# First attention of a two-layer backbone: emptying the value product's bank with two ScalarE copies and two VectorE additions, and taking the reciprocals on GpSimd

## The chip, the cores and the metric

One core of a Trainium2 chip runs the whole program. The metric is the device time of one execution in microseconds (us). The engines are TensorE (PE, with its weight loads shown apart as PEld), VectorE (DVE), ScalarE (ACT), GpSimd (POOL) and SyncE (SP), which issues most of the DMAs. Each engine executes its own list of instructions in order; where an instruction waits for another engine, everything behind it on its list waits too.

## The reference

A backbone of two layers over 1024 latent tokens and 256 context tokens, width 1024, float32. Layer 0 is a windowed attention with 16 query heads in 4 groups and a sink logit for each head, layer 1 a latent attention; each is wrapped in a norm, a modulation and a gated residual. The change lies in layer 0 alone:

```
def attend_block(args):                      # one block of 128 queries
    s_loc = einsum("bqhgd,bkhd->bhgqk", q, k) * scale     # 3 blocks of keys, masked
    s_ctx = einsum("bqhgd,bchd->bhgqc", q, kc) * scale    # 256 context keys
    p = softmax_with_sink(concatenate([s_loc, s_ctx]), sink_b)
    return einsum(p[..., :3 * BLOCK], v) + einsum(p[..., 3 * BLOCK:], vc)
...
yx = (ox * silu(gx)) @ w_out
```

The softmax divides by the sum of the exponentials and the sink's; the kernel does the division after the product with the values.

## The kernel before

Products are made in three passes of split numbers (`split` writes a high and a low part, `mm3` runs high·high, low·high, high·low at L126 to L128). Layer 0's attention works in 40 units, numbered 0 to 39 here: ten tiles of 128 queries (in the order 2, 0, 3, 1, 4, 5, ..., 9, where tiles 0 and 1 are context) times four head groups. A unit has four heads and `m` chunks of 128 keys: 2 for context tiles, 4 for tiles 2 and 9, 5 for the others. The steps of a unit, with the names used below:

- **scores** (`score`, L584 on PE): per head two or four matmuls into one of two bank pairs, (0,1) or (2,3); then on DVE L595 adds the mask and takes the minimum (an instruction "ISA" or CUSTOM_DVE, and a small one that reads its accumulator), and on ACT L598 takes the exponential and the sum of the row.
- **denominators** (`post`, `post2`): L602 on POOL, L603 on ACT, L607 on POOL, the reciprocal L608 on DVE, and L610 on POOL, which spreads the four reciprocals over 256 columns.
- **transposes** of a chunk (`T`, L615 on PE, four of 128x128) into bank 6 or 7, which ACT (cast L121) and DVE (subtraction L122) empty into a high and a low part.
- **value products** (`PV`, L625, two matmuls of 128x512 for each chunk) into bank 5. V holds its high and low part beside each other in the stationary operand, so that the product's upper and lower 64 partitions hold two parts that have to be added. All units use this one bank: `psv = Banks(5)`.
- **emptying the bank** (`fin`): four ACT copies of 64x256 (L635 and L636, twice each) from bank 5 into two buffers, `o` and `o2`.
- **finishing** (`fin2`): two transposes of the spread reciprocals (L644, into bank 0 or 2 by turns: the first bank of a pair of the scores), an ACT copy of them (L646), then on POOL the sum `o + o2` (L648), two multiplications (L649, L650), a cast and a subtraction (L652, L653) that make the operand of the output projection. The last unit does these five on DVE (`fast=True`).
- **output projection** of a finished tile (`outproj`, L126 to L128 into bank 4, DVE L673, POOL L674) is fed between the units' chunks.

What order the instructions take on each engine is set by a scheduler when the program is built: it places each by its priority and its estimate of when operands and banks come free. A later part of the kernel (layer 1's attention) is ordered by hand. Weights of the output projection are loaded and split during the first units (`wo_load`, the casts L121 and subtractions L122 from `arena_f`).

Of the kernel before, what the change touches and what calls it, by code (L numbers as in the profile page):

```python
# [13 lines left out]
ALU = mybir.AluOpType  # L14
# [33 lines left out]
def shp(ap, *dims):  # L48
    n = 1
    for d in dims:  # L50
        n *= d
    ap = ap[:, 0:n]
    if len(dims) == 1:
        return ap
    names = "abcdefg"[: len(dims)]
    kw = {c: d for c, d in zip(names[1:], dims[1:])}
    return ap.rearrange("p (" + " ".join(names) + ") -> p " + " ".join(names), **kw)
# [3 lines left out]
def kernel(ctx: ExitStack, tc: tile.TileContext, t, out, dbg=None):  # L61
    nc = tc.nc
# [6 lines left out]
    F = cpool.tile([128, F_KB * KB], F32, name="arena_f")  # L69
# [26 lines left out]
    def sm(n):  # L96
        o = _so[0]
        _so[0] += n
        assert _so[0] <= 480
        return small[:, o : o + n]  # L100
# [39 lines left out]
    sel2 = sm(2)  # L140
    mhalf = sm(1)
    nc.vector.memset(mhalf, -0.5)
    const = sm(2)
    nc.vector.memset(const[:, 0:1], 1.0)
    nc.vector.memset(const[:, 1:2], 0.0)
# [367 lines left out]
    ytmp = Ring(F, [12], 512)  # L513
    wstg = Ring(F, [4, 6, 12], 512)
    rbr = Ring(F, [42, 47], 256)
    or1, or2, rtr = (Ring(F, [o, o - 5], 256) for o in (43, 44, 45))
    Pr = Ring(F, [14 + 2.5 * i for i in range(8)], 640)
    gr = Ring(F, [2.5, 34, 46], 256)
    xr0 = Ring(F, [4], 1024)
# [22 lines left out]
    class UnitA:  # L542
# [62 lines left out]
        def post2(self):  # L605
            den = self.den
            nc.gpsimd.tensor_add(den, den, self.esk)  # L607
            nc.vector.reciprocal(den, den)  # L608
            self.rb = rbr.next()
            nc.gpsimd.tensor_copy(shp(self.rb, 4, 64), den.unsqueeze(2).to_broadcast([128, 4, 64]))  # L610

# [18 lines left out]
        def fin(self, og):  # L630
            self.og = og
            pvv = self.pv.rearrange("p (j e q) -> p j e q", j=2, e=2)
            o, o2 = shp(or1.next(), 2, 128), shp(or2.next(), 2, 128)
            for e, a, b in ((0, 0, 64), (1, 64, 0)):
                nc.scalar.copy(o[a : a + 64], pvv[b : b + 64, :, e, :])  # L635
                nc.scalar.copy(o2[a : a + 64], pvv[a : a + 64, :, e, :])  # L636
            self.o, self.o2 = o, o2

        def fin2(self, fast=False):
            g, og = self.g, self.og  # L640
            o, o2 = self.o, self.o2
            rt = shp(prt(), 4, 128)
            for j in range(2):
                nc.tensor.transpose(rt[:, j, :], self.rb[:, j * 128 : j * 128 + 128], ident)  # L644
            rs = shp(rtr.next(), 2, 128)
            nc.scalar.copy(rs, rt[:, 0:2, :])  # L646
            eng = nc.vector if fast else nc.gpsimd
            eng.tensor_add(o, o, o2)  # L648
            eng.tensor_mul(rs, rs, self.gt)  # L649
            eng.tensor_mul(o, o, rs)  # L650
            hi = og[:, 0, 2 * g : 2 * g + 2, :]
            eng.tensor_copy(hi, o)  # L652
            eng.tensor_sub(og[:, 1, 2 * g : 2 * g + 2, :], o, hi.bitcast(F32))  # L653
# [1021 lines left out]
```

## Time and profile before

| what | value |
|---|---|
| time, median of 3 runs | 1604.39 us (1603.81 to 1604.47) |
| the profiled execution: its own time | 1606.03 us |
| its span in the trace | 1604.2 us |
| PE busy over the span | 1559.0 us, 97% |
| DVE, ACT, POOL busy | 866.1, 804.6, 734.2 us |
| layer 0's attention, units 0 to 39 | about 360 to 726 us of the span |

A profile row of a group gives the line, the engine, the operation, output <- input by name, shape, count, then busy time and mean duration in ns, then the idle time of the engine just before these instructions and what ended it. A row "X <- Y: a, b, c" of the waits says that X waited for Y for a us in total, b times, c at the longest. In the timeline a row has the start, the duration, the engine, the line and, in brackets, the idle time before it.

### The profile page before, as it was taken

What the parts mean: (1) busy time and instruction counts of PE and PEld (TensorE: products, weight loads), DVE (VectorE), ACT (ScalarE), POOL (GpSimd) and SP (SyncE); (2) the same over time, 40 slices, a digit from 0 to 9 for tenths busy, and PEclk for the clock granted to TensorE, in tenths of its full rate; (3) what the DMA queues carried; (4) which work ended last, traced back from release to release, by engine and by line L of the source; (5) the groups of instructions that cost most, each with busy time, mean ns of one, the idle gap of its engine ahead of it and who ended that gap; (6) DMA issues with size and microseconds to landing.
All of it is one profiled execution on the core that took longest, in us unless ns stands there. A gap on an engine that the chain in (4) does not pass through costs nothing.

```text
span 1604.2 us, 26843 instructions
## 1 busy us (share of the span) xinstructions
PE 1559.0 (97%) x9938; PEld 1226.8 (76%) x9938; DVE 866.1 (54%) x1589; ACT 804.6 (50%) x1558; POOL 734.2 (46%) x804
## 2 busy tenths in 40 slices
PE   7999999998999999998999999999999999999998
PEld 3787777886878888887998899766766766766587
DVE  2515551617666666667624301567666566567354
ACT  3522232349877777777523333355555555555321
POOL 1231121114554444454213340388688688789510
PEclk8999999999999999999999999999999999999999
DMA  7446766354333333317112763313323233244251
GB/s 249 167 140 196 238 201 186 100 148 119 109 109 93 96 93 93 93 57 243 49 41 85 259 198 99 103 30 81 87 82 95 66 96 96 67 128 118 63 169 66
DMA packets 147202, 192.81 MB, mean 120 GB/s; under 512 B 13936, under 2 KB 84080, under 8 KB 147072
## 3 DMA queue, kind: packets, MB, share of 16 engines
q1 hardware_dynamic: 145456, 188.94, 39.5%
q10 hardware_dynamic: 1616, 2.17, 0.4%
q8 instruction: 78, 1.28, 0.4%
q14 instruction: 52, 0.43, 0.1%
HBM read 144.90 MB, written 46.15 MB: 119 GB/s over the span
## 4 chain that ended last, share of the span: by engine, by line
PE 82%; ACT 6%; DVE 3%; issue 2%; POOL 2%; DMA 2%; SPq 0%; POOLq 0%; DVEq 0%; ACTq 0%
PE PB L126 14%; PE PB L127 14%; PE PB L128 14%; PE PB L1302 11%; PE PB L1324 8%; PE PB L1265 4%; PE PB L625 4%; PE PB L615 3%; PE PB L584 3%; ACT arena_r L121 2%; ACT arena_f L636 1%; ACT arena_f L635 1%; PE PB L181 1%; PE PB L1273 1%; ACT arena_f L598 1%
## 5 line engine op out<-in xcount | busy, mean ns | idle before, releaser
L126 PE MATMUL PB<-arena_r 128*128 128x512 f32 (+3 forms) x1496 | 509.6, 342 | 4.2 <-ACT arena_r L387 1.6
L127 PE MATMUL PB<-arena_r 128*128 128x512 f32 (+3 forms) x1496 | 503.1, 336 | 3.7 <-DVE arena_r L388 1.9
L128 PE MATMUL PB<-arena_r 128*128 128x512 f32 (+3 forms) x1496 | 501.2, 335 | 0.4 <-DVE arena_r L122 0.4
L1316 POOL TENSOR_TENSOR arena_f<-arena_f 128x512 f32<-128x512 f32 x252 | 324.6, 1288 | 79.5 <-ACT arena_f L1308 62.7
L126 PEld LDWEIGHTS PB<-arena_r 128*128 128x128 f32 x1496 | 284.0, 190 | 51.5 <-issue 12.5
L127 PEld LDWEIGHTS PB<-arena_r 128*128 128x128 f32 x1496 | 285.1, 191 | 31.4 <-DVE arena_r L388 3.4
L128 PEld LDWEIGHTS PB<-arena_r 128*128 128x128 f32 x1496 | 285.4, 191 | 28.2 <-DVE arena_r L122 0.6
L122 POOL TENSOR_TENSOR arena_r<-arena_f,arena_r 128x512 fp32r<-128x512 f32 x88 | 115.3, 1325 | 302.7 <-ACT arena_r L121 260.9
L1308 ACT ACTIVATE arena_f<-PB 128x1024 f32<-128x1024 f32 x160 | 164.1, 1027 | 108.5 <-PE PB L1302 68.9
L1267 DVE TENSOR_REDUCE arena_f<-PB 128x1 f32<-128x1024 f32 x128 | 156.1, 1219 | 86.6 <-PE PB L1265 86.5
L1302 PE MATMUL PB<-arena_r 64*128 64x512 f32 (+1 forms) x1600 | 202.4, 392 | 0.3 <-ACT arena_f L1308 0.3
L1302 PEld LDWEIGHTS PB<-arena_r 64*128 64x128 f32 (+1 forms) x1600 | 147.1, 185 | 30.6 <-ACT arena_f L1308 1.8
L595 DVE CUSTOM_DVE_ANT_0 arena_f<-PB,arena_f,small 128x640 f32<-128x640 f32 (+2 forms) x176 | 123.7, 721 | 47.6 <-PE PB L584 47.1
L122 DVE TENSOR_TENSOR arena_r<-PB,arena_r 128x512 fp32r<-128x512 f32 (+1 forms) x186 | 123.4, 673 | 39.6 <-ACT arena_r L121 38.2
L1324 PE MATMUL PB<-arena_f 128*64 128x512 f32 x640 | 144.4, 597 | 0.0
L598 ACT ACTIVATE arena_f<-arena_f,small 128x640 f32<-128x640 f32 (+2 forms) x160 | 118.9, 744 | 29.5 <-DVE small L595 28.8
L625 PE MATMUL PB<-arena_r 128*128 128x512 f32 x336 | 124.2, 440 | 8.4 <-ACT arena_f L636 7.8
L121 ACT CAST arena_r<-arena_f 128x512 fp32r<-128x512 f32 (+3 forms) x141 | 83.6, 603 | 89.5 <-DMA arena_f<-b_w_in 12.8
L121 ACT CAST arena_r<-PB 128x512 fp32r<-128x512 f32 (+1 forms) x186 | 104.9, 573 | 31.1 <-PE PB L615 28.8
L584 PE MATMUL PB<-arena_r 128*128 128x256 f32 (+1 forms) x576 | 108.2, 305 | 0.8 <-ACT arena_f L646 0.5
L1324 PEld LDWEIGHTS PB<-arena_f 128*64 128x64 f32 x640 | 43.1, 136 | 83.2 <-issue 79.9
L615 PE MATMUL PB<-ident,arena_f 128*128 128x128 f32 x672 | 105.4, 274 | 0.9 <-ACT arena_f L598 0.5
(178 smaller groups left out, 1836.2 us busy)
## 6 DMA issues: line engine op xcount, KB each, us to landing
arena_f<-ada_w SPq DMA_DIRECT2D x47, 512.0 KB, 5.3
arena_r<-q_d SPq DMA_DIRECT2D x80, 256.0 KB, 3.9
arena_r<-qn_d SPq DMA_DIRECT2D x64, 256.0 KB, 3.9
arena_r<-qr_d SPq DMA_DIRECT2D x192, 64.0 KB, 3.4
arena_f<-a_w_in SPq DMA_DIRECT2D x40, 256.0 KB, 3.4
arena_f<-x SPq DMA_DIRECT2D x16, 512.0 KB, 5.7
g_d<-arena_f SPq DMA_DIRECT2D x32, 256.0 KB, 2.2
q_d<-arena_f SPq DMA_DIRECT2D x64, 128.0 KB, 2.6
```

Source lines behind the costliest of these rows:

```text
L121: nc.scalar.copy(hi, src)
L122: (lo_eng or nc.vector).tensor_sub(lo, src, hi.bitcast(F32))
L126: nc.tensor.matmul(o, ah, bh, start=first, stop=False)
L127: nc.tensor.matmul(o, al, bh, start=False, stop=False)
L128: nc.tensor.matmul(o, ah, bl, start=False, stop=last)
L584: nc.tensor.matmul(S[:, at : at + n], qT[:, s, hq, :], kT[:, g, k : k + n], start=s == 0, stop=s == 1)
L625: nc.tensor.matmul(self.pv, V[:, self.chunks[ci], self.g, :], PT[:, s], start=ci == 0 and s == 0, stop=ci == self.m - 1 and s == 1,)
L1267: nc.vector.reduce_max(mx[:, 32 + b : 33 + b], flat, AX.X, negate=True)
L1302: nc.tensor.matmul(S[:, t], k[r, c : c + 128], q[r], start=j == 0, stop=j == 4)
L1308: nc.scalar.activation(E, self.S, AF.Exp)
L1316: eng.tensor_add(self.acc, self.acc, E[:, t])
L1324: nc.tensor.matmul(self.pv[p : p + 64], Vq[:, cs[t], self.h % 4, :], E[:, t], start=i == 0, stop=i == 4)
```

## The change

The four ACT copies of a unit become two: for the pair of heads `e`, the part of the bank that lies in the other 64 partitions is copied to `o`, and DVE then adds the part that lies in the same partitions onto it, straight from the bank (two additions of 64x256). The buffer `o2` and the POOL sum L648 go. The reciprocal L608 on DVE becomes a power of -1 on POOL, with a column `mone` of -1.

```diff
+    mone = sm(1)
+    nc.vector.memset(mone, -1.0)
...
-    or1, or2, rtr = (Ring(F, [o, o - 5], 256) for o in (43, 44, 45))
+    or1, rtr = (Ring(F, [o, o - 5], 256) for o in (43, 45))
...
             nc.gpsimd.tensor_add(den, den, self.esk)
-            nc.vector.reciprocal(den, den)
+            nc.gpsimd.tensor_tensor(den, den, mone.to_broadcast([128, 4]), ALU.pow)
...
             pvv = self.pv.rearrange("p (j e q) -> p j e q", j=2, e=2)
-            o, o2 = shp(or1.next(), 2, 128), shp(or2.next(), 2, 128)
+            self.o = o = shp(or1.next(), 2, 128)
             for e, a, b in ((0, 0, 64), (1, 64, 0)):
                 nc.scalar.copy(o[a : a + 64], pvv[b : b + 64, :, e, :])
-                nc.scalar.copy(o2[a : a + 64], pvv[a : a + 64, :, e, :])
-            self.o, self.o2 = o, o2
+            for e, a in ((0, 0), (1, 64)):
+                nc.vector.tensor_add(o[a : a + 64], pvv[a : a + 64, :, e, :], o[a : a + 64])
...
-            eng.tensor_add(o, o, o2)
             eng.tensor_mul(rs, rs, self.gt)
             eng.tensor_mul(o, o, rs)
```

In the changed kernel most lines stand two lower: L595 is L597, L584 is L586, L615 is L617, L625 is L627, L644 is L646, L598 is L600, L673 is L674; the copies are L637, the additions L639, the power L610. The scheduler places the instructions of the whole stage anew. Three places follow.

**Place A: from unit 18 to unit 19** (a unit of five chunks; in the trace 517.5 to 519.7 us). PE before, from the second head's scores after the last value product of unit 18 (L584, L615 transposes, L625 the first value product of unit 19, L126 to L128 the output projection, L644 the transposes of the reciprocals):

```order
L584 MATMUL PB<-arena_r 128x256 x2
L584 MATMUL PB<-arena_r 128x384 x2
L615 MATMUL PB<-ident,arena_f 128x128 x4
L625 MATMUL PB<-arena_r 128x512 x2
L126 MATMUL PB<-arena_r 128x512
L127 MATMUL PB<-arena_r 128x512
L128 MATMUL PB<-arena_r 128x512
L644 MATMUL PB<-ident,arena_f 128x128 x2
```

PE now, from the same place:

```order
L586 MATMUL PB<-arena_r 128x256 x2
L586 MATMUL PB<-arena_r 128x384 x2
L617 MATMUL PB<-ident,arena_f 128x128 x4
L126 MATMUL PB<-arena_r 128x512
L127 MATMUL PB<-arena_r 128x512
L128 MATMUL PB<-arena_r 128x512
L126 MATMUL PB<-arena_r 128x512
L127 MATMUL PB<-arena_r 128x512
L627 MATMUL PB<-arena_r 128x512 x2
L128 MATMUL PB<-arena_r 128x512
L586 MATMUL PB<-arena_r 128x256
L646 MATMUL PB<-ident,arena_f 128x128 x2
```

Five matmuls of the output projection moved ahead of unit 19's first value product. DVE at the same place, before (L122 the subtraction of a transposed chunk, then two heads' scores of unit 20, then the next chunk's subtraction):

```order
L122 TENSOR_TENSOR arena_r<-PB,arena_r 128x512
L595 ISA arena_f,small<-PB,arena_f,small 128x640
L595 ISA small 128x1
L595 ISA arena_f,small<-PB,arena_f,small 128x640
L595 ISA small 128x1
L122 TENSOR_TENSOR arena_r<-PB,arena_r 128x512
```

DVE now:

```order
L122 TENSOR_TENSOR arena_r<-PB,arena_r 128x512 x2
L597 ISA arena_f,small<-PB,arena_f,small 128x640
L597 ISA small 128x1
L639 TENSOR_TENSOR arena_f<-PB,arena_f 64x256 x2
L597 ISA arena_f,small<-PB,arena_f,small 128x640
L597 ISA small 128x1
L122 TENSOR_TENSOR arena_r<-PB,arena_r 128x512
```

The two additions stand between the two heads' scores. In the built program only the second of the two copies signals, and the first addition waits for it.

**Place B: from unit 19 to unit 20** (527.8 to 530.1 us). PE before, again from the second head's scores:

```order
L584 MATMUL PB<-arena_r 128x256 x2
L584 MATMUL PB<-arena_r 128x384 x2
L615 MATMUL PB<-ident,arena_f 128x128 x4
L625 MATMUL PB<-arena_r 128x512 x2
L644 MATMUL PB<-ident,arena_f 128x128 x2
L584 MATMUL PB<-arena_r 128x384 x2
L615 MATMUL PB<-ident,arena_f 128x128 x4
```

PE now:

```order
L586 MATMUL PB<-arena_r 128x256 x2
L586 MATMUL PB<-arena_r 128x384 x2
L617 MATMUL PB<-ident,arena_f 128x128 x8
L646 MATMUL PB<-ident,arena_f 128x128 x2
L586 MATMUL PB<-arena_r 128x384 x2
L126 MATMUL PB<-arena_r 128x512
L627 MATMUL PB<-arena_r 128x512 x3
```

Four more transposes, the transposes of the reciprocals, two score matmuls and one of the output projection moved ahead of unit 20's first value product. On DVE the additions stand as at place A: after the first head's scores, ahead of the second's.

**Place C: the end of unit 1** (376 to 382 us). DVE before (L122 from `PB` is a transposed chunk's subtraction, L122 from `arena_f` that of a piece of the output projection's weights; tile 2's scores are taken in two pieces for each head):

```order
L122 TENSOR_TENSOR arena_r<-PB,arena_r 128x512
L595 ISA arena_f,small<-PB,arena_f,small 128x256
L595 ISA small 128x1
L122 TENSOR_TENSOR arena_r<-PB,arena_r 128x512
L595 ISA arena_f,small<-PB,arena_f,small 128x256
L595 ISA small 128x1
L122 TENSOR_TENSOR arena_r<-arena_f,arena_r 128x512 x2
L595 ISA arena_f,small<-PB,arena_f,small 128x256
```

DVE now:

```order
L597 ISA arena_f,small<-PB,arena_f,small 128x256
L597 ISA small 128x1
L639 TENSOR_TENSOR arena_f<-PB,arena_f 64x256 x2
L122 TENSOR_TENSOR arena_r<-arena_f,arena_r 128x512 x2
L597 ISA arena_f,small<-PB,arena_f,small 128x256
L597 ISA small 128x1
L122 TENSOR_TENSOR arena_r<-PB,arena_r 128x512
```

The two subtractions of weights moved ahead of three of unit 3's score pieces and two chunks' subtractions.

More of the change, by code (lines that the diff above doesn't have):

```diff
@@ L632, in fin @@
             pvv = self.pv.rearrange("p (j e q) -> p j e q", j=2, e=2)
-            o, o2 = shp(or1.next(), 2, 128), shp(or2.next(), 2, 128)
+            self.o = o = shp(or1.next(), 2, 128)
             for e, a, b in ((0, 0, 64), (1, 64, 0)):
                 nc.scalar.copy(o[a : a + 64], pvv[b : b + 64, :, e, :])
-                nc.scalar.copy(o2[a : a + 64], pvv[a : a + 64, :, e, :])
-            self.o, self.o2 = o, o2
+            for e, a in ((0, 0), (1, 64)):
+                nc.vector.tensor_add(o[a : a + 64], pvv[a : a + 64, :, e, :], o[a : a + 64])
         def fin2(self, fast=False):
             g, og = self.g, self.og
-            o, o2 = self.o, self.o2
+            o = self.o
             rt = shp(prt(), 4, 128)
```

## The prediction

> **What bounds the kernel now.** First the page's busy times and its chain: PE is the bound, and the changed work stands nowhere on the chain but in small shares.
>
> ```profile
> PE 1559.0 (97%) x9938; PEld 1226.8 (76%) x9938; DVE 866.1 (54%) x1589; ACT 804.6 (50%) x1558; POOL 734.2 (46%) x804
> PE 82%; ACT 6%; DVE 3%; issue 2%; POOL 2%; DMA 2%; SPq 0%; POOLq 0%; DVEq 0%; ACTq 0%
> ```
>
> So a gain can come only out of time in which PE waits. Next the stage by windows (us, then busy time of PE, PEld, DVE, ACT, POOL): 370 to 400 are the units of the first tile, 400 to 490 short and long units mixed, 490 to 695 the five tiles with units of five chunks.
>
> ```profile
> 370.00:400.00 30.00, 25.79 (x148) 19.21 (x147) 21.44 (x65) 27.39 (x78) 16.86 (x33) 1.00 0.37 107
> 400.00:490.00 90.00, 86.00 (x493) 70.81 (x494) 56.06 (x140) 71.18 (x190) 52.43 (x95) 1.00 0.38 107
> 490.00:695.00 205.00, 201.63 (x1209) 174.04 (x1208) 139.59 (x291) 161.54 (x383) 94.75 (x170) 1.00 0.33 93
> ```
>
> PE leaves 12 us in all; ACT is at 91%, 79% and 79%, DVE at 71%, 62% and 68%. Then the waits, over the stage:
>
> ```profile
> POOL arena_f L648 <- ACT arena_f L636: 60.9, 38, 3.4
> DVE small L608 <- POOL small L607: 31.5, 19, 3.4
> PEld PB L625 <- ACT arena_f L636: 15.1, 26, 1.2
> PE PB L625 <- ACT arena_f L636: 7.8, 22, 0.9
> ```
>
> The wait that matters is PE's: the next unit's first value product (L625) waits until ACT's fourth copy has emptied bank 5. The weight load's 15.1 us is the truer size, since its row starts when the wait ends, while the matmul's rows have modelled ends. By window it is 2.5, 4.9 and 6.9 us:
>
> ```profile
> PEld PB L625 <- ACT arena_f L636: 2.5, 4, 0.8
> ```
>
> ```profile
> PEld PB L625 <- ACT arena_f L636: 4.9, 6, 1.2
> ```
>
> ```profile
> PEld PB L625 <- ACT arena_f L636: 6.9, 15, 0.7
> ```
>
> POOL's 60.9 us and DVE's 31.5 us of waiting hold nothing of PE directly.
>
> **The parts of the change.** Their prices, from the groups (the last two rows are nearest relatives, a DVE operation of 64x256 out of PSUM, and a power on POOL of one column):
>
> ```profile
> L635 ACT COPY arena_f<-PB 64x256 f32<-64x256 f32 x80 | 29.4, 368 | 3.7 <-PE PB L625 2.2
> L636 ACT COPY arena_f<-PB 64x256 f32<-64x256 f32 x80 | 29.4, 368 | 1.2
> L648 POOL TENSOR_TENSOR arena_f<-arena_f 128x256 f32<-128x256 f32 x39 | 28.8, 738 | 63.4 <-ACT arena_f L636 60.9 <-DMA arena_r<-q_d 2.5
> L608 DVE RECIPROCAL small<-small 128x4 f32<-128x4 f32 x40 | 7.0, 176 | 31.5 <-POOL small L607 31.5
> L602 POOL TENSOR_TENSOR small<-small 128x4 f32<-128x4 f32 x40 | 8.2, 206 | 13.7 <-DVE small L595 13.7
> L1227 DVE TENSOR_TENSOR arena_r<-PB,arena_r 64x256 fp32r<-64x256 f32 x32 | 13.5, 422 | 3.7 <-ACT arena_r L1229 2.5
> L214 POOL TENSOR_TENSOR small<-small 128x1 f32<-128x1 f32 x10 | 6.1, 609 | 12.4 <-DVE small L213 11.5 <-DVE small L958 0.8
> ```
>
> ACT loses 80 copies of 0.368, 29.4 us. DVE gains 80 additions of 0.422 by L1227, 33.8 us, and loses 40 reciprocals, 7.0 us, with the waits in front of them. POOL loses 39 sums, 28.8 us, and gains 40 powers. None of this is PE's time; over 490 to 695 ACT falls to about 72% and DVE rises to about 75% (20 units: -0.74, and +0.84 -0.18 each), both still under PE's 98%.
>
> The power on four columns is in no row. Below it is bounded by L602's 0.206 (the same shape, a subtraction), above by four times L214's 0.609, 2.4 us; I take 0.8, a little over one column's, since L602 shows that four columns need not cost four times. It delays L610, and with it the transposes L644. At place A L610 of unit 19 starts at 517.08 and its transposes at 530.62 (rows below), 13 us later; for the short unit 4 it is 5 us:
>
> ```profile
> 396.11 0.40 POOL L610 COPY arena_f<-small 128x256 f32<-128x256 f32 x1
> ```
>
> ```profile
> 401.56 0.38 PE L644 MATMUL PB<-ident,arena_f 128*128 128x128 f32 x2
> ```
>
> So on PE it costs nothing. On SP the load of a tile's x goes behind some loads of q; no wait of the stage names either on PE.
>
> The bank is what decides. Place A, the rows of the trace:
>
> ```profile
> 517.08 0.40 POOL L610 COPY arena_f<-small 128x256 f32<-128x256 f32 x1 [1.60 <-DVE small L608]
> ...
> 518.11 0.37 ACT L635 COPY arena_f<-PB 64x256 f32<-64x256 f32 x1
> ...
> 518.49 0.37 ACT L636 COPY arena_f<-PB 64x256 f32<-64x256 f32 x1
> 518.72 0.88 DVE L595 CUSTOM_DVE_ANT_0 arena_f<-PB,arena_f,small 128x640 f32<-128x640 f32 x1
> 518.76 0.53 PEld L615 LDWEIGHTS PB<-ident,arena_f 128*128 128x128 f32 x4
> ...
> 519.25 0.37 ACT L636 COPY arena_f<-PB 64x256 f32<-64x256 f32 x1
> 519.52 0.08 DVE L595 DVE_READ_ACCUMULATOR2_ANT small<- 128x1 f32 x1
> ...
> 519.66 0.30 PEld L625 LDWEIGHTS PB<-arena_r 128*128 128x128 f32 x2 [0.38 <-ACT arena_f L636]
> ...
> 520.24 0.39 PE L126 MATMUL PB<-arena_r 128*128 128x512 f32 x1
> ...
> 520.47 0.40 PE L127 MATMUL PB<-arena_r 128*128 128x512 f32 x1
> ```
>
> The fourth copy ends at 519.62 and PE goes on 0.04 to 0.05 later: that is a handover. PE had been ready at 519.29 (518.76 + 0.53). Now: both copies end at 518.86, earlier than the additions can begin, because DVE is in the first head's scores until 519.60 (519.52 + 0.08). The additions run to 519.60 + 2 x 0.42 = 520.44, the bank is free at 520.49. In front of the product PE now has five matmuls of 0.23 (L126 to L127 in the rows): 519.29 + 1.15 = 520.44. It waits 0.05 instead of 0.38, and the five matmuls are work it needn't do later: 0.33 gained. Note that the bank itself comes free 0.87 later than before; the gain is in the order of PE, not in the bank.
>
> Place B:
>
> ```profile
> 528.99 0.54 PEld L615 LDWEIGHTS PB<-ident,arena_f 128*128 128x128 f32 x4
> ...
> 530.01 0.08 DVE L595 DVE_READ_ACCUMULATOR2_ANT small<- 128x1 f32 x1
> ...
> 530.04 0.30 PEld L625 LDWEIGHTS PB<-arena_r 128*128 128x128 f32 x2 [0.51 <-ACT arena_f L636]
> ...
> 530.50 0.83 ACT L598 ACTIVATE arena_f<-arena_f,small 128x640 f32<-128x640 f32 x1
> 530.62 0.38 PE L644 MATMUL PB<-ident,arena_f 128*128 128x128 f32 x2
> ```
>
> DVE leaves the first head's scores at 530.09, the additions end at 530.93, the bank is free at 530.98. PE, ready at 529.53, now has four transposes (0.54, to 530.07), then L644's two, whose bank 2 the same scores hold until 530.14: a new wait of 0.07. They take about 0.22, two score matmuls 0.36, one of the projection 0.23: 530.95, and a wait of 0.03. Behind the product, two score matmuls need bank 2 again, so they wait for ACT to copy L644's result, now behind a cast and one exponential of 0.83: worked through, another 0.19. So 0.51 - 0.07 - 0.03 - 0.19 = 0.22 gained. The third wait of a tile (0.43, from unit 17 to 18) is in its order like B; at B's ratio it gives 0.18. Per tile 0.33 + 0.22 + 0.18 = 0.73 of 1.32, 55%; of the 6.9 us in 490 to 695 that is **3.8 us**.
>
> In 400 to 490 two of six waits hold nearly half of the time, and there the bank is late because ACT comes late to the copies; then the additions come later still. I take half of the ratio: 0.28 x 4.9, **1.4 us**. In 370 to 400 I take **0**, between two ends: all of the 2.5 us gained with ACT at 91% relieved, or at place C a loss. There DVE's subtractions of weights,
>
> ```profile
> 379.52 0.69 DVE L122 TENSOR_TENSOR arena_r<-arena_f,arena_r 128x512 fp32r<-128x512 f32 x1 [1.08 <-ACT arena_r L121]
> 380.56 1.37 DVE L122 TENSOR_TENSOR arena_r<-arena_f,arena_r 128x512 fp32r<-128x512 f32 x1 [0.35 <-ACT arena_r L121]
> ```
>
> 2.1 us of work that before followed three score pieces of unit 3, now precede them, right behind additions that wait for both copies. PE then waits for these scores (L584's bank) up to 2 us, perhaps twice: -4. In 695 to 730 the one wait of 0.83 (unit 38 to 39) is covered by two more projection matmuls, **0.3**. At the end of the stage ACT gets from two copies fewer, 0.74 us, earlier to the first norm of layer 1, whose result PE awaits:
>
> ```profile
> 729.73 0.86 PEld L222 LDWEIGHTS PB<-ident,arena_f 128*128 128x128 f32 x8 [1.19 <-DVE small L213]
> ```
>
> I count half, **0.4**, since a weight's DMA follows on ACT. After that nothing changes in the order, and a PE bound part keeps what it is given. Sum: 3.8 + 1.4 + 0 + 0.3 + 0.4 = 5.9 us. The profiled execution (1606.03, its span 1604.2) would come to 1600.1; it stands 1.6 above the median of 1604.39, from which the forecast is **1598.5**.
>
> **The rivals.** *No change* (within 0.2%, 3.2 us, about what this measurement can tell): the wait moves from the bank to L644's bank, to the scores' banks and to the chunks' subtractions behind the additions. B shows three quarters of the way to it: the 5.9 shrinks under 3.2 if place A's kind is like B's and the first tile costs 2. Time 1602.5.
>
> *Slower*, by DVE at the bank: additions run only when both copies are done and DVE is free. From rows, with a free DVE the bank takes 2 x 0.37 + 2 x 0.42 + two handovers, 1.69, against 1.51 (518.11 to 519.62) before; behind one more head's scores 0.88 comes on top. PE's added cover is 1.15 at A and 1.4 at B, and the additions use 0.87 of it; if DVE is late by 0.9 in most units (contention, or additions of 0.69 like full rows), 28 units times some 0.4 bring 11 us, 1610. It decides from about 0.3 us of lateness per unit on. Against it: DVE loses 31.5 us of waiting for L607.
>
> The Trainium skill, "PSUM — Partial Sum Buffer", section "PSUM bank collisions raise a hardware error", says that reads by ScalarE and VectorE of one bank and quadrant must not overlap either. By that rule the serial 1.69 holds wherever DVE is free, which speaks against the change; at A and B it alters nothing, since DVE comes free only after the second copy. Without it a first addition could start behind the first copy, and the bank would take 0.37 + 0.84 + 0.05 = 1.26 where DVE is free. No trace here shows two engines in one bank at once, which agrees and does not test it.
>
> *More*: ACT's relief in 370 to 490 clears those waits and the others there, and all 15.1 + 0.74 us go: 1588.5 at the end, 1592 in the middle.
>
> **How the numbers follow.** Forecast 0.48 (1594 to 1601.2), more 0.15 (below 1594), no change 0.25 (1601.2 to 1607.6), slower 0.12 (above). Faster is 0.63, same 0.25, slower 0.12. The range leaves out about 0.07 below and 0.13 above: 1592 to 1606.
>
> **What would show it.** Right: L625's weight load waits some 8 us in all instead of 15.1, now for DVE's additions; new short waits of L644 for the scores' reduction; no DVE wait for L607; ACT about 72%, DVE about 75% in the middle tiles; L639 near 0.42; the power near 0.8. Wrong: additions well above 0.42 or released late by DVE; waits of PE in the first tile above 4 us for scores; a power near 2.4, with L644 waiting for POOL.

## The result, and the profile after

The changed kernel takes 1597.9 us (median of 6 runs, 1596.15 to 1600.38) against 1604.43 us for the kernel before (6 runs, 1602.2 to 1606.1): ratio 0.996, 95% interval [0.9947, 0.9973], some 6.5 us faster. A second comparison, on another chip, gave 1599.3 against 1603.72 us, ratio 0.9969 [0.9956, 0.9981]. The profiled execution took 1596.15 us, its span is 1594.4 us.

First the page's busy times and its chain, as shown of before:

```profile
PE 1555.2 (98%) x9938; PEld 1222.6 (77%) x9938; DVE 905.9 (57%) x1629; ACT 777.0 (49%) x1478; POOL 742.1 (47%) x805
PE 86%; issue 2%; DVE 2%; POOL 2%; ACT 2%; DMA 1%; SPq 0%; POOLq 0%; DVEq 0%; ACTq 0%
```

PE does the same work; ACT's share of the chain fell from 6% to 2%. By windows (busy time of PE, PEld, DVE, ACT, POOL):

```profile
370.00:400.00 30.00, 25.75 (x148) 19.29 (x147) 24.10 (x70) 24.54 (x69) 17.43 (x33) 1.00 0.39 106
400.00:490.00 90.00, 88.35 (x515) 73.88 (x516) 66.06 (x156) 66.02 (x173) 57.89 (x101) 1.00 0.40 113
490.00:695.00 205.00, 204.46 (x1228) 175.82 (x1227) 156.80 (x318) 149.47 (x349) 101.09 (x173) 1.00 0.32 93
```

From 490 to 695 PE now leaves 0.5 us instead of 3.4 (and runs 1228 matmuls there instead of 1209), from 400 to 490 1.7 instead of 4.0; from 370 to 400 it leaves as much as before. The waits of the stage that have to do with PE, and POOL's longest:

```profile
POOL arena_f L650 <- ACT arena_f L648: 111.9, 34, 6.4
PEld PB L646 <- issue: 4.8, 21, 0.3
PEld PB L586 <- DVE small L597: 3.5, 8, 1.7
PEld PB L126 <- POOL arena_r L653: 2.6, 2, 1.7
PEld PB L627 <- issue: 2.3, 9, 0.4
PEld PB L127 <- POOL arena_r L654: 1.4, 2, 0.9
```

The 15.1 us for the fourth copy are gone, and no wait of that size took their place on PE. POOL's multiplication now waits 111.9 us for L648's copy, where its sum waited 60.9 for the bank's last copy. The new instructions, by groups:

```profile
L610 POOL TENSOR_TENSOR small<-small 128x4 f32<-128x4 f32 x40 | 40.5, 1013 | 2.5
L639 DVE TENSOR_TENSOR arena_f<-PB,arena_f 64x256 f32<-64x256 f32 x80 | 33.6, 420 | 2.0 <-ACT arena_f L637 0.9
L637 ACT COPY arena_f<-PB 64x256 f32<-64x256 f32 x80 | 29.3, 367 | 3.8 <-PE PB L627 2.4
```

For the stage alone one row is enough, the value products by line: their shortest, median and longest duration, then the first and the last start. Before and after:

```profile
L625 PE MATMUL PB<-arena_r x336: 387/473/507, 362.6 to 723.4; 128*128 128x512 f32 x168
```

```profile
L627 PE MATMUL PB<-arena_r x336: 387/397/499, 362.2 to 715.9; 128*128 128x512 f32 x168
```

From the first value product to the last it is 360.8 us before and 353.7 after: 7.1 us less. This length is called "the stage" below. It is free of what varies from run to run at the program's start and at the entry of layer 1, some 1 to 3 us each. In the second comparison's profile it is 355.3, but there the granted TensorE clock (the column behind POOL's: 0.83 here, 1.00 for the same window of the first profile) fell for a moment:

```profile
395.00:405.00 10.00, 8.32 (x39) 6.29 (x38) 4.78 (x14) 5.94 (x18) 7.39 (x14) 0.83 0.31 81
```

Value products took up to 776 ns there (at most 499 in the first profile), and from unit 5's first value product to unit 6's it took 7.0 us instead of 5.4. That is the whole difference of 1.6 us; in the rest of the stage the two profiles agree within 0.1 us.

### The profile page after: what moved, and what is told of

Its sections match the earlier page's. It is cut to its first block, busy times and chain, and to the rows that moved or that the text cites. A ratio compares the mean times of both kernels' runs of the same rounds, so it can differ in the third digit from the quotient of the medians.

```text
span 1594.4 us, 26916 instructions
## 1 busy us (share of the span) xinstructions
PE 1555.2 (98%) x9938; PEld 1222.6 (77%) x9938; DVE 905.9 (57%) x1629; ACT 777.0 (49%) x1478; POOL 742.1 (47%) x805
## 4 chain that ended last, share of the span: by engine, by line
PE 86%; issue 2%; DVE 2%; POOL 2%; ACT 2%; DMA 1%; SPq 0%; POOLq 0%; DVEq 0%; ACTq 0%
PE PB L126 15%; PE PB L127 14%; PE PB L128 14%; PE PB L1303 11%; PE PB L1325 8%; PE PB L586 5%; PE PB L627 4%; PE PB L1266 4%; PE PB L617 4%; PE PB L183 1%; PE PB L1274 1%; PE PB L1354 1%; PE PB L646 1%; ACT arena_r L121 1%; DVE arena_r L122 1%
## 5 line engine op out<-in xcount | busy, mean ns | idle before, releaser
L126 PE MATMUL PB<-arena_r 128*128 128x512 f32 (+3 forms) x1496 | 509.9, 342 | 4.9 <-POOL arena_r L653 2.0
L127 PE MATMUL PB<-arena_r 128*128 128x512 f32 (+3 forms) x1496 | 502.4, 336 | 4.2 <-DVE arena_r L390 2.1
L128 PE MATMUL PB<-arena_r 128*128 128x512 f32 (+3 forms) x1496 | 500.3, 335 | 0.3 <-DVE arena_r L122 0.3
L1317 POOL TENSOR_TENSOR arena_f<-arena_f 128x512 f32<-128x512 f32 x252 | 328.3, 1303 | 82.1 <-ACT arena_f L1309 65.3
L126 PEld LDWEIGHTS PB<-arena_r 128*128 128x128 f32 x1496 | 283.7, 190 | 52.7 <-issue 12.5
L127 PEld LDWEIGHTS PB<-arena_r 128*128 128x128 f32 x1496 | 284.5, 190 | 32.0 <-DVE arena_r L390 3.5
L128 PEld LDWEIGHTS PB<-arena_r 128*128 128x128 f32 x1496 | 284.5, 190 | 28.3 <-DVE arena_r L122 0.5
L122 POOL TENSOR_TENSOR arena_r<-arena_f,arena_r 128x512 fp32r<-128x512 f32 x88 | 115.2, 1325 | 299.7 <-ACT arena_r L121 255.5
L1303 PEld LDWEIGHTS PB<-arena_r 64*128 64x128 f32 (+1 forms) x1600 | 146.1, 185 | 31.5 <-ACT arena_f L1309 1.8
L122 DVE TENSOR_TENSOR arena_r<-PB,arena_r 128x512 fp32r<-128x512 f32 (+1 forms) x186 | 124.2, 674 | 61.9 <-ACT arena_r L121 61.0
L600 ACT ACTIVATE arena_f<-arena_f,small 128x640 f32<-128x640 f32 (+2 forms) x160 | 119.5, 747 | 35.4 <-DVE small L597 32.7
L597 DVE CUSTOM_DVE_ANT_0 arena_f<-PB,arena_f,small 128x640 f32<-128x640 f32 (+2 forms) x176 | 125.2, 722 | 20.1 <-PE PB L586 12.6
L627 PE MATMUL PB<-arena_r 128*128 128x512 f32 x336 | 115.8, 429 | 0.5 <-DVE arena_f L639 0.5
L586 PE MATMUL PB<-arena_r 128*128 128x256 f32 (+1 forms) x576 | 111.0, 308 | 1.6 <-DVE small L597 1.3
L617 PE MATMUL PB<-ident,arena_f 128*128 128x128 f32 x672 | 104.2, 274 | 1.3 <-DVE arena_r L122 0.8
```

Of the source, the lines that this page charges most:

```text
L122: (lo_eng or nc.vector).tensor_sub(lo, src, hi.bitcast(F32))
L126: nc.tensor.matmul(o, ah, bh, start=first, stop=False)
L127: nc.tensor.matmul(o, al, bh, start=False, stop=False)
L128: nc.tensor.matmul(o, ah, bl, start=False, stop=last)
L586: nc.tensor.matmul(S[:, at : at + n], qT[:, s, hq, :], kT[:, g, k : k + n], start=s == 0, stop=s == 1)
L617: nc.tensor.transpose(pt[:, h, :], self.Ps[h][:, ci * 128 : ci * 128 + 128], ident)
```

## The experiments

| kernel | median, us | ratio to before, 95% interval | stage, us |
|---|---|---|---|
| before | 1604.4 | | 360.8 |
| changed, first and second time | 1597.9, 1599.3 | 0.996 [0.9947, 0.9973], 0.9969 [0.9956, 0.9981] | 353.7, 355.3 |
| PE's order alone | 1607.3 | 1.0022 [1.0013, 1.0031] | 363.8 |
| the instructions alone, PE's order of before | 1622.9 | 1.0116 [1.0102, 1.013] | 379.4 |
| PE's and ACT's order | 1598.5 | 0.9965 [0.9953, 0.9978] | 354.5 |
| PE's, ACT's and DVE's order | 1596.9 | 0.9956 [0.9944, 0.9969] | 353.8 |
| reciprocal alone | 1604.0 | 0.9997 [0.9988, 1.0007] | 361.2 |
| additions alone, first and second time | 1594.7, 1595.8 | 0.9944 [0.9931, 0.9957], 0.9949 [0.9936, 0.9963] | 352.7, 352.9 |
| power from the third tile on | 1595.3 | 0.9944 [0.9931, 0.9956] | 351.9 |
| additions alone, weights' subtractions on POOL | 1595.5 | 0.9949 [0.9937, 0.9962] | 351.4 |
| copies alone | 1591.2 | 0.9921 [0.9907, 0.9934] | 348.1 |
| additions alone, off the bank | 1596.5 | 0.9945 [0.9931, 0.9958] | 352.6 |

The stage is read from one profile each. Those of the changed kernel's second time and of the reciprocal alone (granted clock 0.91 from 380 to 400 us) hold such a fall of the clock; the others do not.

### Order and instructions apart

The prediction's main step says that the gain is in the order of PE and not in the bank. Both kernels issue the same instructions on PE, and of the stage's 2144 only 584 stand at another place. So an order can be given to the other kernel, by edges between consecutive instructions of one engine that set the order of issue and wait for nothing:

```diff
+PE0, PEN = 1718, 2681
+PE_ORDER = [
...
+    pe = [i for i in nc.cur_bb.bb.instructions if i.engine == E.PE][PE0 : PE0 + PEN]
+    order = [pe[k] for s, n in PE_ORDER for k in range(s, s + n)]
+    no_sync = mybir.DependencyInfo(mybir.DependencyClass.NoSync, mybir.DependencyReason.DATA)
+    for x, y in zip(order, order[1:]):
+        tc.add_manual_dep(y, x.name, no_sync, reason="order")
```

**PE's order alone**, in before:

> The instructions of before (four ACT copies, the POOL sum, DVE's reciprocal), but PE is given, instruction for instruction, the order that it has in the changed kernel; the other engines' orders are placed anew around it. Theory (the gain is the order of PE, more work ahead of a unit's first value product): the whole gain is there without the change, 1596 to 1599 us, with L625's weight load waiting under 5 us in the stage instead of 15.1; since the bank comes free 0.87 us earlier than in the changed kernel, it may be the faster of the two by up to 1 us. Rival 1 (ACT's relief of 29 us, or DVE's, or POOL's, makes the gain): as before, 1603 to 1606 us. Rival 2 (both needed): about 1601 us.

Measured 1607.3 us: the theory as it stood there falls. The table of numbers at the file's head moves the lines: value products are L672, copies L682 and L683, scores L631, exponentials L645, the copy of the transposed reciprocals L693. The bank's wait did go (0.7 us of L672's weight load for L683), and another came, the weight load's waits over the stage:

```profile
PEld PB L631 <- ACT arena_f L693: 15.5, 16, 1.8
PEld PB L662 <- DVE arena_r L169: 4.5, 11, 0.7
```

The timeline shows it at place B, ACT from the end of unit 19 on (start, duration):

```profile
529.26 0.37 ACT L682 COPY arena_f<-PB 64x256 f32<-64x256 f32 x1
...
530.40 0.37 ACT L683 COPY arena_f<-PB 64x256 f32<-64x256 f32 x1
530.79 0.58 ACT L168 CAST arena_r<-PB 128x512 fp32r<-128x512 f32 x1
531.28 0.83 ACT L645 ACTIVATE arena_f<-arena_f,small 128x640 f32<-128x640 f32 x1
...
532.10 0.82 ACT L645 ACTIVATE arena_f<-arena_f,small 128x640 f32<-128x640 f32 x1
...
532.91 0.35 ACT L693 COPY arena_f<-PB 128x256 f32<-128x256 f32 x1
```

and the score matmul that waits for it:

```profile
533.32 0.30 PEld L631 LDWEIGHTS PB<-arena_r 128*128 128x128 f32 x2 [1.04 <-ACT arena_f L693]
```

Two exponentials stand ahead of the copy that frees the scores' bank. In before they stood there too, but PE came to these scores later. In the changed kernel one exponential stands there.

**The instructions alone**: the changed kernel with PE's order of before.

> The instructions of the changed kernel, but PE keeps, instruction for instruction, the order that it has in before. Theory: the bank comes free some 0.85 us later at each unit (two additions behind a head's scores) and PE has nothing more to put in front of the value product, so the wait of L627 grows from 15.1 us by 25 to 30 units times 0.5 to 0.85: 1616 to 1628 us, slower than before. Rival 1 (relief of ACT, DVE and POOL makes the gain): 1597 to 1601 us, as the changed kernel. Rival 2 (both needed): about 1602 to 1606 us.

Measured 1622.9 us, as the theory has it. The value products are L665 here, the additions L677; the group of their weight loads, before and here, and the matmuls' wait:

```profile
L625 PEld LDWEIGHTS PB<-arena_r 128*128 128x128 f32 x336 | 53.0, 191 | 16.1 <-ACT arena_f L636 15.1 <-ACT arena_r L121 0.6
```

```profile
L665 PEld LDWEIGHTS PB<-arena_r 128*128 128x128 f32 x328 | 51.5, 190 | 30.9 <-ACT arena_r L159 23.6 <-ACT arena_f L638 6.7
```

```profile
PE PB L665 <- DVE arena_f L677: 24.3, 25, 1.5
```

The weight loads' idle time doubled, 16.1 to 30.9 us (up to 735 us of the span). The weight load's row names casts and exponentials, the matmul's the additions. The change's instructions in PE's old order are a loss of 18.5 us: PE comes to the bank as early as before, and the bank comes free later.

**All three orders**, in before. The changed kernel's order of ACT and DVE is given too; POOL's order and the place of the reciprocals are left to the scheduler:

> The instructions of before once more, now with the changed kernel's order on PE, ACT and DVE (the two further copies follow their neighbours; the reciprocals are placed freely). Beside the order of PE this puts L646's copy, which frees the scores' bank, ahead of the second of two exponentials on ACT; with PE's order alone it stood behind both, and the scores waited 15.5 us for it. Theory (the gain is the order on two engines, not the work that the change takes away): 1594 to 1598 us, with the score matmuls' wait for that copy under 3 us and the value products' wait for the bank under 2 us. Rival (ACT needs the 0.77 us that a unit's two copies take, or POOL the sum's time): 1600 to 1606 us, with the score matmuls still waiting 8 us or more for that copy.

Measured 1596.9 us, stage 353.8 (changed: 353.7). Here the copies are L745 and L746, the exponentials L708, the copy of the reciprocals L756, the scores L694. Place B again:

```profile
525.51 0.37 ACT L745 COPY arena_f<-PB 64x256 f32<-64x256 f32 x1
...
526.65 0.37 ACT L746 COPY arena_f<-PB 64x256 f32<-64x256 f32 x1
527.04 0.59 ACT L231 CAST arena_r<-PB 128x512 fp32r<-128x512 f32 x1
527.52 0.83 ACT L708 ACTIVATE arena_f<-arena_f,small 128x640 f32<-128x640 f32 x1
...
528.35 0.36 ACT L756 COPY arena_f<-PB 128x256 f32<-128x256 f32 x1
```

From the first copy to L756 it is 2.84 us instead of 3.65, with all four copies still there. PE's busy time in the middle tiles is that of the changed kernel:

```profile
490.00:695.00 205.00, 204.54 (x1238) 177.98 (x1237) 143.49 (x301) 166.37 (x395) 97.65 (x177) 1.00 0.33 95
```

ACT is at 81% (166.37 of 205), and in these tiles it costs nothing: the relief of ACT, of POOL's sum and of DVE's reciprocal isn't needed for the gain there. The 4.8 us that the scores still wait for L756 are more than the 3 us expected.

**PE's and ACT's order**, DVE's left to the scheduler:

> The instructions of before with the changed kernel's order on PE and ACT; DVE's order is left to the scheduler (with all three orders it was 1596.9 us, with PE's alone 1607.3). Theory: what was missing with PE's order alone is the place of L646's copy on ACT, one exponential earlier; DVE's order adds little: 1596 to 1599 us, and the score matmuls no longer wait for that copy. Rival (DVE's order, that is which head's scores it reduces when, is what counts): 1602 to 1607 us.

Measured 1598.5 us, stage 354.5: within the measurement the same. ACT's order is what was missing. ACT's order without PE's was not run.

The equal totals hide two different gains. The stage in three parts, by the starts of the first value products of units 0, 16 and 36 and of the last value product (us):

| kernel | units 0 to 15 | 16 to 35 | from 36 on |
|---|---|---|---|
| before | 126.6 | 204.1 | 30.2 |
| changed, first; second time | 123.9; 125.5 | 200.8; 200.8 | 29.0; 29.1 |
| PE's order alone | 127.5 | 207.0 | 29.3 |
| all three orders | 126.2 | 199.0 | 28.6 |
| PE's and ACT's order | 126.4 | 199.0 | 29.1 |
| additions alone, first time | 122.8 | 201.0 | 28.9 |
| copies alone | 118.6 | 199.6 | 30.0 |
| additions alone, off the bank | 121.7 | 200.3 | 30.5 |

In the middle tiles the old instructions in the new order gain more than the change does, 5.1 us against 3.3, though PE's busy time is the same; the number of matmuls in the window (1238 against 1228) shows it. In units 0 to 15 they gain 0.4 us where the change gains 2.7. So the order explains the gain of the middle tiles. For the first sixteen units no run tells whether the relief of ACT or POOL gains the rest, or the orders that were left to the scheduler.

### The parts of the change

**The additions alone**:

```diff
-            nc.gpsimd.tensor_tensor(den, den, mone.to_broadcast([128, 4]), ALU.pow)
+            nc.vector.reciprocal(den, den)
```

> Two copies and two additions as in the changed kernel, the reciprocal back on DVE. The scheduler gives PE nearly the order of the changed kernel (109 of the stage's 2144 instructions stand elsewhere, against 584 between before and after). Theory: nearly the whole gain, 1597 to 1600 us; the power on POOL is worth 0 to 1 us. Rival (the reciprocal's leaving DVE, with 31.5 us of waiting for POOL's L607, makes the gain): 1602 to 1606 us.

> The additions alone once more, beside the next two kernels. 1594 to 1596 us if the 1594.65 of the first time holds; 1596 to 1598 us if it was the chip's.

Measured 1594.7 and 1595.8 us, below the 1597 to 1600 of the first expectation: all of the gain, and some 3 us more.

**The reciprocal alone**: before with the power on POOL.

> The reciprocal as a power on POOL, the four copies and the POOL sum kept. PE's order is nearly that of before (138 instructions stand elsewhere). Theory: no gain that can be measured, 1602.5 to 1605.5 us, with L625's weight load still waiting 13 us or more. Rival (DVE's waits for L607 were what made the bank or the scores late): 1597 to 1600 us.

Measured 1604.0 us, stage 361.2, the bank's wait as expected (L627 is the value product, L638 the last copy):

```profile
PEld PB L627 <- ACT arena_f L638: 13.1, 26, 0.8
```

On balance DVE's 31.5 us of waiting for POOL were worth nothing; from unit 16 to 36 it is 204.1 us, as before.

**The changed kernel once more**, beside the orders:

> The changed kernel beside the additions alone, which measured 1594.65 us in another call. If the power on POOL costs nothing, as the prediction has it, 1594 to 1597 us, and the 1597.9 of the first comparison was the chip's; if it costs some 3 us, 1597 to 1599 us.

Measured 1599.3 us, the upper case, just past its end: the power costs. Where shows POOL's timeline in the changed kernel, at the end of a unit of the first two tiles:

```profile
395.95 0.74 POOL L651 TENSOR_TENSOR arena_f<-arena_f 128x256 f32<-128x256 f32 x1
396.65 1.99 POOL L610 TENSOR_TENSOR small<-small 128x4 f32<-128x4 f32 x2
398.59 0.40 POOL L653 CAST arena_r<-arena_f 128x256 fp32r<-128x256 f32 x1
...
399.29 0.73 POOL L654 TENSOR_TENSOR arena_r<-arena_f,arena_r 128x256 fp32r<-128x256 f32 x1
```

Two powers stand between the multiplication and the cast that makes the projection's operand, and PE waits for that cast:

```profile
399.04 0.19 PEld L126 LDWEIGHTS PB<-arena_r 128*128 128x128 f32 x1 [1.71 <-POOL arena_r L653]
```

With the additions alone the cast follows the same multiplication at once:

```profile
396.75 0.74 POOL L651 TENSOR_TENSOR arena_f<-arena_f 128x256 f32<-128x256 f32 x1
397.55 0.40 POOL L653 CAST arena_r<-arena_f 128x256 fp32r<-128x256 f32 x1
```

and of the waits of L126 for L653 and of L127 for L654, 2.6 and 1.4 us in the changed kernel, 0.2 us is left with the additions alone:

```profile
PEld PB L126 <- POOL arena_r L653: 0.2, 1, 0.2
```

Before had these waits too (its lines are one lower):

```profile
PEld PB L126 <- POOL arena_r L652: 2.0, 2, 1.3
PEld PB L127 <- POOL arena_r L653: 1.2, 2, 0.6
```

With the additions alone, where POOL's sum is gone, they are nearly gone too; with the power they are back. So the next kernel has the power only from the third tile on:

```diff
-            nc.gpsimd.tensor_tensor(den, den, mone.to_broadcast([128, 4]), ALU.pow)
+            if self.ti in ORDER[:2]:
+                nc.vector.reciprocal(den, den)
+            else:
+                nc.gpsimd.tensor_tensor(den, den, mone.to_broadcast([128, 4]), ALU.pow)
```

> The changed kernel with the reciprocal on DVE in the first two tiles (units 0 to 7) and the power on POOL in the eight others; PE's order is, instruction for instruction, that of the additions alone. Theory: the power costs PE time only in the first two tiles, where the projection waits for POOL's last steps (2.6 us for L653 and 1.4 us for L654 in the changed kernel), so this is as fast as the additions alone, 1594 to 1596 us. Rival (the power costs everywhere, 32 units of 1.0 us on POOL): 1597 to 1599 us.

Measured 1595.3 us: as fast as the additions alone beside it (1595.8). The power's cost lies in the first two tiles; 32 powers behind them cost nothing. PE's order differs there too between the changed kernel and the additions alone (377 to 407 us), so POOL's queue and the order are not told apart. Of the some 3 us between the medians the stage shows about 1 (353.7 against 352.7 and 352.9, in profiles without a fall of the clock); the rest wasn't located. The changed kernel and the additions alone were each measured beside before, not beside each other.

### What the additions themselves cost

**Copies alone**: before with two of the four copies and the POOL sum left out, so that one part of the product is missing.

```diff
-                nc.scalar.copy(o2[a : a + 64], pvv[a : a + 64, :, e, :])
...
-            eng.tensor_add(o, o, o2)
```

> Before with the copies of L636 and the sum L648 left out (the part of the product in the same partitions is never added): the bank is free after two copies, 0.75 us sooner than before and some 1.6 us sooner than in the changed kernel; ACT and POOL have the same relief as in the changed kernel, DVE does nothing for it. PE's order is neither kernel's (384 instructions of the stage stand elsewhere than before). By the order theory: 1593 to 1599 us, within 3 us of the additions alone, since there the late bank was already covered. Rival (the additions cost PE time through DVE or the late bank): 1588 to 1592 us, clearly below the additions alone.

Measured 1591.2 us, the rival's range: without additions it would be 4 us faster than the additions alone. Most of that lies early. From the first value product of unit 0 to that of unit 8 it is 53.1 us here, 57.3 with the additions alone (55.9 with them off the bank, the next run), 58.6 before; the middle tiles give another 1.4 us (199.6 against 201.0), and the last units lose 1.1. Two reasons were left, the bank's later release and DVE's time. The last run gives the bank its early release back: DVE adds a constant from SBUF, and one part of the product is again missing.

```diff
-                nc.vector.tensor_add(o[a : a + 64], pvv[a : a + 64, :, e, :], o[a : a + 64])
+                nc.vector.tensor_add(o[a : a + 64], shp(mask, 2, 128)[a : a + 64], o[a : a + 64])
```

> The additions alone, but DVE adds a constant from SBUF (the mask's first columns) instead of the bank's second part, which is never read: DVE has the same two instructions a unit, ACT and POOL the same relief, and the bank is free after the two copies, as with the copies alone (1591.2 us; the additions alone 1594.7 and 1595.8). The scheduler places PE anew. Theory 1 (DVE's 34 us of additions are what the additions alone lose on the copies alone, through the scores' reductions and the chunks' subtractions behind them): 1594 to 1596.5 us. Theory 2 (the bank's later release, and the order that follows from it, is what is lost): 1590.5 to 1592.5 us.

Measured 1596.5 us at the end of theory 1's range; the stage, 352.6, is that of the additions alone and not the 348.1 of the copies alone:

```profile
L627 PE MATMUL PB<-arena_r x336: 387/473/505, 364.0 to 716.6; 128*128 128x512 f32 x168
```

```profile
L625 PE MATMUL PB<-arena_r x336: 387/473/525, 361.6 to 709.7; 128*128 128x512 f32 x168
```

(the first row of this kernel, the second of the copies alone). So in sum the early release is worth nothing once DVE has the two instructions. On the way it is worth 1.8 us of the 5.7 that the copies alone are ahead at unit 36, and behind unit 36 it is lost again, in an order of its own; the additions also take longer here, 0.448 us instead of 0.420. Whether they cost by their time or by the order that the scheduler makes around them, these two runs don't tell. An attempt to win it back by relieving DVE otherwise:

```diff
-        engs = [nc.gpsimd, nc.vector]
+        engs = [nc.gpsimd, nc.gpsimd]
```

> The additions alone, with all subtractions of the output projection's weights on POOL instead of every other on DVE: three fewer of some 0.9 us on DVE in 355 to 420 us, where DVE is at 87%, three more of 1.3 us on POOL. By the theory that DVE's load in the first tile is what keeps the additions alone some 3.5 us above the copies alone: 1591 to 1593.5 us. Rival (POOL's last steps come later and the projection waits for them, or the late bank itself costs): 1594.5 to 1598 us.

Measured 1595.5 us, beside 1595.8 for the additions alone: nothing that can be measured, though the stage is 1.4 us shorter. The 1591 to 1593.5 that DVE's load in the first tile would have given isn't reached. (The 87% of the expectation is DVE's share from 370 to 400 us; from 355 to 420 it is 75%.) The best of the complete kernels are thus the additions alone and its two variants, about 1595 us, and the simplest of them is the change without its power.

## Why the prediction was right, and where it was off

The time came out at the forecast, 1597.9 for 1598.5. The terms, by the starts of the first value products of units 16, 36 and 39 in the profiled execution and in that of the second comparison, each against the one profile of before (the last term up to 795 us, from where the kernels run alike):

| term | forecast | first | second |
|---|---|---|---|
| 370 to 490 (units 0 to 15) | 1.4 | 2.7 | 1.1 |
| 490 to 695 (units 16 to 35) | 3.8 | 3.3 | 3.3 |
| 695 to 730 | 0.3 | 0.7 | 0.6 |
| end of the stage, entry of layer 1 | 0.4 | 3.0 | 0.9 |
| sum | 5.9 | 9.6 | 5.8 |

The second's 1.1 holds the 1.6 us of the low clock; without it, it would be 2.7 as in the first. The last 3.0 and 0.9 aren't the change's alone either: from 725 to 795 us the granted clock is 0.95 in the profile of before, 0.98 in the first and 0.95 in the second. And the first profile is of the fastest of its six runs, so its sum is above the 6.5 us of the medians.

That the sum came out so near is partly luck. Units 0 to 15 gained about twice their term, and the power, which has no term, took some 3 us away: without it the gain is 9.7 and 8.9 us.

**The order, not the bank**: right for the middle tiles, from which 3.8 of the 5.9 us were to come, and there shown from both sides; the same order with the old instructions gains 5.1 us, and the new instructions in PE's old order lose 13.7. For the first sixteen units it isn't shown. It was incomplete in one thing. The working at place B counted the copy of the reciprocals "behind a cast and one exponential", and took that for given; it is a second move, on ACT, without which PE's order is a loss of 3 us.

**Place A** came nearly as worked out:

```profile
513.77 0.75 ACT L637 COPY arena_f<-PB 64x256 f32<-64x256 f32 x2
```

```profile
515.19 0.85 DVE L639 TENSOR_TENSOR arena_f<-PB,arena_f 64x256 f32<-64x256 f32 x2
```

```profile
515.68 0.19 PEld L127 LDWEIGHTS PB<-arena_r 128*128 128x128 f32 x1
516.16 0.30 PEld L627 LDWEIGHTS PB<-arena_r 128*128 128x128 f32 x2 [0.29 <-issue]
```

The additions end 2.27 us after the copies began (2.33 forecast), and the product's weights go in 2.39 after (2.38). That the second is nearer than the first is chance: the step from the additions' end to the weights took 0.12, not the 0.05 of the forecast (see the end). The weight load's wait is 0.29 us, but in PE's own rows

```profile
515.68 0.40 PE L126 MATMUL PB<-arena_r 128*128 128x512 f32 x1
515.92 0.39 PE L127 MATMUL PB<-arena_r 128*128 128x512 f32 x1
516.19 0.70 PE L627 MATMUL PB<-arena_r 128*128 128x512 f32 x2
```

the product starts 0.27 after the projection's last matmul, and these follow each other every 0.24: PE lost 0.03, near the forecast's 0.05. Here "the truer size" of the prediction, the weight load's wait, overstates, because a matmul runs beside it. Over the five middle tiles the gain was 0.65 for each instead of 0.73.

**Place B** came near as well. The weight loads' waits there are 0.21 in front of L646 (0.07 forecast) and 0.12 in front of the product (0.03), and behind the copy of the reciprocals, which ends at 526.89, the scores' weights go in at 526.95, 0.04 after PE was free (0.19 forecast); in sum 0.37 instead of 0.29:

```profile
525.60 0.20 PEld L646 LDWEIGHTS PB<-ident,arena_f 128*128 128x128 f32 x2 [0.21 <-issue]
...
526.37 0.54 PEld L627 LDWEIGHTS PB<-arena_r 128*128 128x128 f32 x3
```

**Place C** didn't cost what was feared. Up to unit 4's first value product the changed kernel takes 32.9 us where before took 32.7, near the 0 that was taken, and up to 396 us PE's weight loads wait 0.2 us for the scores' reduction.

**The waits that were forecast**: L627's weight load idles 6.5 us in the stage (some 8 forecast), but the rows name "issue", casts and exponentials, not DVE's additions:

```profile
L627 PEld LDWEIGHTS PB<-arena_r 128*128 128x128 f32 x336 | 52.8, 190 | 6.5 <-issue 2.3 <-ACT arena_r L121 1.1 <-ACT arena_f L600 0.9
```

What speaks for the additions all the same: in 30 of the 39 changes of unit the first weight load starts 0.09 to 0.13 us after the second addition's end, as at place A, whatever stands ahead of it. L646 waits 4.8 us in 21 pieces, "issue" again where the scores' reduction was forecast. ACT is at 73% and DVE at 76% in the middle tiles (72 and 75), L639 takes 0.420 (0.42). No DVE wait for the denominators is left.

**The step that failed** is the power: "So on PE it costs nothing". Its size was near (1.01 us, 0.8 taken), but only the transposes L646 were looked at, which read its result. What stands behind it on POOL, the cast and the subtraction that make the projection's operand, wasn't; in the first two tiles PE waits 4.0 us for them, 0.2 without the power. Without it the same change gains some 9 us; how much of the difference is these waits and how much the other order of PE there stays open.

**The rivals**: "more" was that ACT's relief clears the waits. The relief is worth nothing in the middle tiles (all three orders, ACT at 81%); in units 0 to 15 it may be worth something, since the copies alone gain 8.0 us there and the three orders 0.4, but the copies alone also have an order of their own and the earlier bank. "No change" has in PE's order alone the very mechanism that it named, the wait moving to the scores' bank, at 15.5 us. "Slower by DVE at the bank" is the instructions alone: 25 waits, up to 1.5 us, for the additions. In the middle tiles, what decides between these and the forecast is the order that the scheduler makes.

## What to carry to other kernels

Where a scheduler sets the order, a change of instructions is two changes, and they can be of opposite sign: pin each kernel's order onto the other's instructions, on every engine that frees a buffer and not on PE alone, before crediting the instructions. Compare such kernels stretch by stretch: two equal totals hid a gain that lies in other places. An operation moved to an idle engine must be followed through that engine's queue: what stands behind it, and who waits for that, as well as who reads it. The parts of a change are worth running apart: here the half that looked harmless cost some 3 of 9 us.

## What the runs showed that was not expected

From the end of DVE's second addition to PE's weight load it is 0.12 us (place A: 516.04 to 516.16), against 0.05 from ACT's last copy before. That isn't DVE's doing. In the changed kernel an instruction of its own, which only waits, stands in PE's queue ahead of 30 of the products' weight loads; before has none there:

```profile
L627 PEldq EVENT_SEMAPHORE  x30: 51/51/51, 372.0 to 712.1; - x30
```

It starts 0.04 us after the addition's end and takes 0.051, and in 26 of the 30 the weight load goes in 0.03 later. Where a weight load of the same trace waits for DVE without such an instruction, it goes in 0.05 us after DVE's end, in all 21 such waits of over 0.1 us in the stage. So what adds some 0.06 us is the wait instruction, not the engine. Such an instruction also stands directly ahead of all 9 loads of L627 and all 21 of L646 whose waits the rows put to "issue".

A power of 128x4 on POOL takes 1.013 us where the subtraction of the same shape takes 0.205: five times as long.
